# Memory tiles 4 to 15 in strips, statistics summed from strips, natural x loaded in layer 0, and a ring of six raw weight buffers

## The chip, the cores and the metric

The kernel runs on one core of one Trainium2 chip. A time is device microseconds of one execution; for the kernel before, the median of three runs is given. Shares and starts inside an execution come from one profiled execution of the same kernel, whose times are counted from the start of its span.

## The reference

Two layers of a bidirectional encoder trunk, on x of 256 tokens by 2048 and a memory of 256 tokens by 2048, all in float32:

```
for l in 0, 1:
    h    = rmsnorm(x, norm_g[l])
    proj = h @ w_in[l]                        # 2048 x 7168, split into three groups of heads
    y_a  = short gated convolution of proj's first 3072 columns
    y_d  = differential attention, 6 heads, of the next 3072 columns
    mn   = rmsnorm(mem, mem_norm_g[l])
    mkv  = mn @ w_mem_kv[l]                   # 2048 x 1024: memory keys and values
    y_m  = attention of the last 1024 columns' queries over the 256 memory tokens, gated
    x    = x + concat(y_a, y_d, y_m) @ w_out[l]
```

Two things matter for the change. The products with w_mem_kv of both layers need the memory once, transposed (contraction index on the partitions), and they don't depend on x; the kernel makes them first. And each rmsnorm needs a sum of squares per token, of mem once and of x once per layer. The kernel folds the norm's gain into the operand and applies the token's scale to the product, so these sums are needed only after the products.

## The kernel before

Every float32 product is made of three products of split operands: a number is taken apart into a high part (`hi`, in TensorE's float32r format) and the rest (`lo`), and hi*hi, hi*lo and lo*hi are accumulated in PSUM. ScalarE makes `hi` (a copy with a scale), VectorE makes `lo` (a subtraction).

**The memory stage** is the first part of the program. It has 32 steps `g`, 16 contraction tiles `k` of 128 rows for each of the two layers. A step needs 512 KB of raw weights (`weights(g)`), split by `w_parts(g)`, and for the first 16 steps the memory's tile k transposed and split into `memT` by `token_parts(g)`; `memT` is kept for layer 1's steps. `products(g, half, which)` issues twelve matmuls of 128x128x512 per step (L827): two halves (keys, values), two token blocks, three part pairs. `FIRST` is hi*hi, `REST` the other two. At step g the operands of step g + 2 are made (L942), and `beside(g)` (L856) issues loads and side work.

- Tiles 0 to 7 (`DEALT = 8`) are loaded in natural layout into `xs` (`tokens`, L774) and transposed on TensorE against an identity (`turned`, L795), two 128x128 transposes a tile.
- Tiles 8 to 15 are loaded as strips, in pieces of 512 bytes (`strips_of`, L676), four at a time, and transposed by VectorE in 32x32 blocks, one instruction of 128x1024 for four tiles (`strips_turned`, L686). The same half of mem is also loaded in natural layout, for the squares alone.
- Raw weights go through a ring of four buffers (L780): the load of step g + 4 waits until VectorE has made `lo` of step g.
- x is loaded twice in this stage: as strips for the transposed `xT` of layer 0 (`x_turned`, L692), and in natural layout (`x_natural`, L847), which gives the squares (`x_square`, L722) and is the residual to which layer 0 adds its output.
- Squares are ScalarE activations of 128x512 with an accumulated sum (`mem_squares`, L731).

**The order.** Instructions wrapped in `pin` keep the program's order on their engine; the others are placed by a planner from its own estimates. Loads go through the sync queue (SP) in order: one that waits for its buffer holds those behind it. Side work is a list of generators, `tasks`; `run_side` is called once per step or per chunk of two contraction tiles, and resumes each generator when its due chunk has come (`yield 2` means two chunks later). At the end of the stage `empty_keys` (L833) copies the keys' accumulators away on ScalarE (L836), which frees PSUM for layer 0.

**The layers.** `block` (L293) makes 16 contraction tiles of 512 columns of w_in or w_out; `load_w` (L280) has its own loads and splits (L285, L289, L290), its matmuls are L310 to L312. Blocks 0 to 5 of a layer give queries, keys, values and gate of the differential attention. From the end of block 4 on, attention runs in pairs of heads beside the blocks (`pair`, L539): scores (L593, L594), softmax, a transpose that ends with a trip through DRAM (`carry`, L424), and the product with the values (L480).

Of the kernel before, what the change touches and what calls it, by code (L numbers as in the profile page):

```python
# [19 lines left out]
P = 128  # L20
# [19 lines left out]
QT = NB // P  # L40
DEALT = 8

# [7 lines left out]
def encoder(ctx: ExitStack, tc: tile.TileContext, x, mem, norm_g, w_in, conv_w, conv_b,  # L50
# [54 lines left out]
    def small_loads():  # L105

        for m in range(DEPTH):
            yield gm_dealt[:, m], mem_norm_g[m, DEALT * P:].rearrange("(q p j) -> p q j", p=P, j=QT)
# [22 lines left out]

    gm_dealt = const.tile([P, DEPTH, (KT - DEALT) // QT, QT], F32, name="gm_dealt")

    def g_mnorm(l, k):
        if k < DEALT:
            return cva[:, l * KT + k:l * KT + k + 1]
        q, j = divmod(k - DEALT, QT)
        return gm_dealt[:, l, q, j:j + 1]

# [535 lines left out]

    def strips_of(src, at_once=1):  # L676

        st = tmp.tile([P, SEQ // B, B * QT], F32, tag="e", name=nm("xt"))
        for b in range(NA):
            pin(nc.sync.dma_start(  # L680
                st[b * B:(b + 1) * B], src[:, b * B * QT:(b + 1) * B * QT].rearrange("(n p) r -> p n r", p=B)))
            if (b + 1) % at_once == 0 and b + 1 < NA:
                yield
        return st

    def strips_turned(st):  # L686
        whole = tmp.tile([P, QT, SEQ], F32, tag="sh", name=nm("xf"))
        pin(nc.vector.transpose(whole.rearrange("p j (n i) -> p j n i", i=B),  # L688
                                st.rearrange("p n (c j) -> p j n c", j=QT)))
        return whole  # L690

    def x_turned(dst, l, q, src, at_once):  # L692


        st = yield from strips_of(src, at_once)
        yield 2
        whole = strips_turned(st)
        yield
        for j in range(QT):
            split_T(dst, q * QT + j, whole[:, j], g_norm(l, q * QT + j), pin=True)  # L700
            if j % 2:
                yield

    def x_next(dst, l, q):

        d = dram.tile([NT, P, NB], F32, name=nm("xd"))
        tc.keep_in_program_order(nc.sync.dma_start(d.rearrange("t p c -> p t c"), xs[:, :, q * NB:(q + 1) * NB]))
        yield 2
        yield from x_turned(dst, l, q, d.rearrange("t p c -> (t p) c"), NA)

# [17 lines left out]
    memT = T_tile("memT")  # L728
    ssm = const.tile([P, NT, 4], F32, name="ssm")

    def mem_squares(c):  # L731

        for t in range(NT):
            sq = tmp.tile([P, NB], F32, tag="nat", name=nm("msq"), bufs=3)
            pin(nc.scalar.activation(sq, xs[:, t, c * NB:(c + 1) * NB], AF.Square, accum_out=ssm[:, t, c:c + 1]))

    def keys(l, nat):
# [21 lines left out]
    def mem_stats():  # L759

        vec = Steps()
        t = small.tile([P, NT], F32, tag="ssum", name=nm("ssum"))
        vec.tensor_reduce(t, ssm, AX.X, ALU.add)
# [13 lines left out]
    def weights(g, at=0, n=2 * NB, eng=nc.sync):  # L777
        l, k = divmod(g, KT)
        if g not in raws:
            raws[g] = wp.tile([P, CK, NB], F32, tag="raw", name=nm("raw"), bufs=4)  # L780
        if k < DEALT:
            rows = w_mem_kv[l][k * P:(k + 1) * P]
        else:
            rows = x_row_tiles(w_mem_kv[l], k - k % CK)[:, k % CK]
        pin(eng.dma_start(raws[g].rearrange("p h c -> p (h c)")[:, at:at + n], rows[:, at:at + n]))

    def w_parts(g, at=0, n=2 * NB):
# [4 lines left out]
        pin(nc.scalar.activation(hi, raw, AF.Copy, scale=gain))  # L792
        pin(nc.vector.scalar_tensor_tensor(lo, raw, gain, hi.bitcast(F32), ALU.mult, ALU.subtract))  # L793

# [7 lines left out]

    def mem_turned(q, at_once):
        st = yield from strips_of(mem[:, q * NB:(q + 1) * NB], at_once)
        yield 2
        dealt[q] = strips_turned(st)

# [4 lines left out]
    def operands(g):  # L812
        token_parts(g)
        w_parts(g)

# [30 lines left out]

    def x_natural(c, t):  # L847
        pin(nc.sync.dma_start(xs[:, t, c * NB:(c + 1) * NB], x[t * P:(t + 1) * P, c * NB:(c + 1) * NB]))

    TOKENS = {0: 4, 1: 6, 8: 8, 9: 10, 10: 12, 11: 14}  # L850
    MEM_STRIPS = {2: 2, 4: 3}
    X_STRIPS = {12: 0, 16: 1, 20: 2, 24: 3}
    X_NATURAL = {14: (0, 0), 17: (0, 1), 20: (1, 0), 22: (1, 1), 24: (2, 0), 26: (2, 1), 28: (3, 0), 29: (3, 1)}
    X_SQUARES = {19: 0, 25: 1, 29: 2}

    def beside(g):  # L856


        if g + 4 < NG:
            if g in TOKENS:  # L860
                tokens(TOKENS[g], 2)
            weights(g + 4)
        if g in MEM_STRIPS:
            tasks.append(later(mem_turned(MEM_STRIPS[g], 2 if g == 2 else 1), 1))
        if g >= 2:
            for dst, src in islice(constants, 1):
                pin(nc.sync.dma_start(dst, src))
        if g in X_STRIPS:
            q = X_STRIPS[g]
            tasks.append(later(x_turned(xT, 0, q, x[:, q * NB:(q + 1) * NB], 1), 1))  # L870
# [8 lines left out]
        if g in X_NATURAL:  # L879
            x_natural(*X_NATURAL[g])  # L880
        if g in X_SQUARES:
            for t in range(NT):
                x_square(X_SQUARES[g], t)

    row_sums = []

    def last_square():
        for t in range(NT):
            x_square(3, t)
        yield 2  # L890
        row_sums.append(stats_of(ssx, "st"))

# [10 lines left out]
    weights(1, NB, NB)  # L903
    tokens(2, 1)
    weights(2, 0, NB)
    weights(2, NB, NB)
    tokens(3, 1)
    weights(3)
    warm(6)
    distance(0)  # L910
# [44 lines left out]
    empty_values(1)  # L955
    tasks.append(later(last_square(), 2))
    for l in range(DEPTH):
# [18 lines left out]
        for b in order:  # L976
# [185 lines left out]
```

## Time and profile before

| | |
|---|---|
| median of three runs | 918.13 us (918.06 to 918.37) |
| profiled execution, its own time | 918.26 us |
| its span | 916.5 us |
| TensorE matmul busy | 912.1 us, 4167 instructions |
| TensorE weight load busy | 758.0 us |
| VectorE busy | 682.3 us |
| ScalarE busy | 512.4 us |
| read from HBM | 194.32 MB, 235 GB/s over the span |

The busy time of TensorE counts overlapping matmuls once each as a stretch from start to modelled end, so 100% doesn't say that no time was lost between their starts; for that one looks at when successive matmuls begin. In rows of the profile, `L827 PE MATMUL acc<-hi,memT 128*128 128x512` is a matmul of the program's line 827 that writes tile `acc` from `hi` and `memT`; `x12` counts instructions; a bracket at the end gives the engine's idle time before it and what ended it. PE is TensorE, PEld its weight loads, DVE VectorE, ACT ScalarE, SP the sync engine with the loads' queue; a q behind a name means its instruction queue.

### The profile page before, as it was taken

To read this page: it belongs to the slowest core of one execution; us is meant where nothing else is said; L and a number is where in the kernel's file an instruction comes from. 1 tells how busy PE (TensorE), PEld (TensorE's weight loads), DVE (VectorE), ACT (ScalarE), POOL (GpSimd) and SP (SyncE) were. 2 spreads that over 40 slices of the span, in tenths; PEclk is the share of its full clock that TensorE was granted. 3 is DMA by queue.
4 is the path that set the end of the run, shared out by engine and by line. 5 is a ranking of instruction groups with operands and counts; after the bars stand their busy time and mean duration, and the time that the engine had idled before them with its cause. 6 is when DMAs were issued, how large, how long until landed. Compare 5 with 4: busy or idle time off the path is not lost.

```text
span 916.5 us, 12329 instructions
## 1 busy us (share of the span) xinstructions
PE 912.1 (100%) x4167; PEld 758.0 (83%) x4167; DVE 682.3 (74%) x1216; ACT 512.4 (56%) x802; POOL 7.0 (1%) x18
## 2 busy tenths in 40 slices
PE   9999999999999999999999999999999999999998
PEld 7888888888888888888888888888888888888887
DVE  5888978857897787658677757878899786658553
ACT  6766745675554765545455544568555664446431
POOL 0001000000000000000000000000000000000000
PEclk9999999999999999999999999999999999999999
DMA  9999888876769989978687867886888979978662
GB/s 286 291 270 310 273 253 235 254 211 185 187 212 239 247 249 266 264 255 249 214 257 249 237 195 221 235 237 176 242 231 222 254 206 260 288 228 241 210 216 80
DMA packets 252964, 216.11 MB, mean 236 GB/s; under 512 B 131727, under 2 KB 180197, under 8 KB 252901
## 3 DMA queue, kind: packets, MB, share of 16 engines
q1 hardware_dynamic: 250740, 211.78, 80.5%
q0 software_dynamic: 672, 2.10, 0.6%
q10 hardware_dynamic: 1488, 1.46, 0.5%
q8 instruction: 32, 0.52, 0.2%
q14 instruction: 32, 0.25, 0.1%
HBM read 194.32 MB, written 20.97 MB: 235 GB/s over the span
## 4 chain that ended last, share of the span: by engine, by line
PE 91%; DMA 4%; DVE 2%; ACT 1%; issue 1%; SPq 0%; ACTq 0%; DVEq 0%
PE acc L311 29%; PE acc L310 29%; PE acc L312 29%; DMA raw<-in_w_mem_kv_dram 3%; PE po L480 1%; PE acc L827 1%; DMA raw<-in_w_in_dram 1%; DVE xf L688 1%; DVE lo L793 1%; ACT hi L792 1%; PE poT L469 1%; PE s L594 1%; PE s L593 1%; PE s L646 1%; DMA xt<-in_mem_dram 0%
## 5 line engine op out<-in xcount | busy, mean ns | idle before, releaser
L290 DVE TENSOR_TENSOR lo<-raw,hi 128x1024 fp32r<-128x1024 f32 x288 | 351.4, 1222 | 171.0 <-ACT hi L289 167.5
L289 ACT CAST hi<-raw 128x1024 fp32r<-128x1024 f32 x288 | 302.2, 1052 | 305.5 <-PE acc L312 235.9
L311 PE MATMUL acc<-lo,xT 128*128 128x512 f32 x896 | 349.2, 390 | 0.0
L312 PE MATMUL acc<-hi,xT 128*128 128x512 f32 x896 | 348.7, 389 | 0.0
L310 PE MATMUL acc<-hi,xT 128*128 128x512 f32 x896 | 347.7, 390 | 0.2 <-ACT kraw L836 0.2
L312 PEld LDWEIGHTS acc<-hi,xT 128*128 128x128 f32 x896 | 168.2, 188 | 34.7
L310 PEld LDWEIGHTS acc<-hi,xT 128*128 128x128 f32 x896 | 168.2, 188 | 34.7 <-ACT kraw L836 0.6
L311 PEld LDWEIGHTS acc<-lo,xT 128*128 128x128 f32 x896 | 168.3, 188 | 33.7
L312 PE MATMUL acc<-hi,yT 128*128 128x512 f32 (+1 forms) x258 | 100.0, 387 | 0.0
L310 PE MATMUL acc<-hi,yT 128*128 128x512 f32 (+1 forms) x258 | 100.0, 387 | 0.0
L311 PE MATMUL acc<-lo,yT 128*128 128x512 f32 (+1 forms) x258 | 99.9, 387 | 0.0
L827 PE MATMUL acc<-hi,memT 128*128 128x512 f32 (+1 forms) x260 | 70.5, 389 | 0.0
L310 PEld LDWEIGHTS acc<-hi,yT 128*128 128x128 f32 x258 | 48.4, 188 | 10.0
L311 PEld LDWEIGHTS acc<-lo,yT 128*128 128x128 f32 x258 | 48.4, 188 | 9.9
L312 PEld LDWEIGHTS acc<-hi,yT 128*128 128x128 f32 x258 | 48.4, 188 | 9.8
L827 PEld LDWEIGHTS acc<-hi,memT 128*128 128x128 f32 x260 | 47.9, 188 | 9.8 <-ACT hi L792 0.3
L827 PE MATMUL acc<-lo,memT 128*128 128x512 f32 (+1 forms) x130 | 39.7, 387 | 0.0
L827 PEld LDWEIGHTS acc<-lo,memT 128*128 128x128 f32 x130 | 24.3, 188 | 5.0
L793 DVE SCALAR_TENSOR_TENSOR lo<-raw,cva,hi 128x1024 fp32r<-128x1024 f32 (+2 forms) x21 | 21.4, 1026 | 6.5 <-ACT hi L792 5.4
L604 ACT ACTIVATE e<-e,mx 128x256 f32<-128x256 f32 x48 | 23.8, 498 | 1.4 <-DVE mx L600 1.3
L793 DVE SCALAR_TENSOR_TENSOR lo<-raw,gm_dealt,hi 128x1024 fp32r<-128x1024 f32 x16 | 20.5, 1279 | 4.6 <-ACT hi L792 4.5
L792 ACT ACTIVATE hi<-raw,cva 128x1024 fp32r<-128x1024 f32 (+2 forms) x21 | 19.7, 947 | 6.4 <-DMA raw<-in_w_mem_kv_dram 6.4
(162 smaller groups left out, 654.6 us busy)
## 6 DMA issues: line engine op xcount, KB each, us to landing
raw<-in_w_in_dram SPq DMA_DIRECT2D x192, 512.0 KB, 4.4
raw<-in_w_out_dram SPq DMA_DIRECT2D x64, 512.0 KB, 4.7
raw<-in_w_in_dram SPq DMA_DIRECT2D x64, 256.0 KB, 4.8
raw<-in_w_mem_kv_dram SPq DMA_DIRECT2D x29, 512.0 KB, 7.1
d<-sh SPq DMA_DIRECT2D x88, 128.0 KB, 3.9
sh<-d SPq DMA_DIRECT2D x72, 128.0 KB, 3.9
xt<-in_x_dram SPq DMA_DIRECT2D x16, 128.0 KB, 6.7
xs<-in_x_dram SPq DMA_DIRECT2D x8, 256.0 KB, 6.8
```

What stands on the lines that cost most here:

```text
L289: nc.scalar.copy(hi, raw)
L290: nc.vector.tensor_tensor(lo_, raw, hi.bitcast(F32), ALU.subtract)
L310: nc.tensor.matmul(acc[t], sh, hi, start=first, stop=False)
L311: nc.tensor.matmul(acc[t], sh, lo, start=False, stop=False)
L312: nc.tensor.matmul(acc[t], sl, hi, start=False, stop=last)
L469: nc.tensor.matmul(po, vp[:, v_part, k], e[:, e_part, k], start=k + v_part + e_part == 0, stop=k == NT - 1 and v_part == 1)
L480: nc.tensor.matmul(po[:, t, :], eT[:, i, t, k, :], v[:, k, h * P:(h + 1) * P], start=k == 0, stop=k == NT - 1)
L593: nc.tensor.matmul(s[c][:, i, :], qi, k_first(yT, c, h), start=True, stop=False)
L604: nc.scalar.activation(e[:, c, i], e[:, c, i], AF.Exp, bias=mx[:, c, i:i + 1], accum_out=sm[:, c, i:i + 1])
L792: pin(nc.scalar.activation(hi, raw, AF.Copy, scale=gain))
L793: pin(nc.vector.scalar_tensor_tensor(lo, raw, gain, hi.bitcast(F32), ALU.mult, ALU.subtract))
L827: pin(nc.tensor.matmul(accs[l, half][t][:, at:at + n], memT[:, token_part, k, t * P:(t + 1) * P], p, start=k == 0 and at == 0 and token_pa ...
```

## The change

- Only tiles 0 to 3 are transposed on TensorE (`DEALT = 4`). Tiles 4 to 7 come as two pairs of strips, in pieces of 256 bytes (`mem_pair`), tiles 8 to 15 as strips of 512-byte pieces as before. VectorE turns the strips tile by tile (`mem_turn`), called from `w_parts` between its `hi` and its `lo`; `token_parts` of a tile now follows its `w_parts`. Strips are loaded into parts of `xs`.
- Natural rows of mem are loaded for tiles 0 to 3 alone; the other squares are taken from the strips, in activations of 128x128 (`strip_squares`), whose sums are spread over partitions and brought together by 16 small copies on VectorE (`folded`). x's squares for layer 0 are made in the same way.
- The raw weights of the memory stage go through six buffers: two are the homes of tiles that layer 0 uses later (`mqT`, `mga`). The load of step g + 6 waits for `lo` of step g.
- x's strips start at steps 9, 13, 17 and 21 instead of 12, 16, 20 and 24, are turned in two halves, and x's natural rows are loaded from the end of block 4 of layer 0, eight loads of 256 KB, one every second chunk.
- The gains of tiles 4 to 15 come as rows dealt to partitions; the first of these small loads is issued before the stage's loop.

```diff
-DEALT = 8
+DEALT = 4
+PAIRED = 8
+RING = 6
...
-    def strips_turned(st):
-        whole = tmp.tile([P, QT, SEQ], F32, tag="sh", name=nm("xf"))
+    def turn_strips(whole, st, at, n, of=QT):
         pin(nc.vector.transpose(whole.rearrange("p j (n i) -> p j n i", i=B),
-                                st.rearrange("p n (c j) -> p j n c", j=QT)))
-        return whole
+                                st.rearrange("p n (c j) -> p j n c", j=of)[:, at:at + n]))
...
+    def strip_squares(which, q, st, ns):
+        for n in ns:
+            v = st(n)
+            sq = tmp.tile([P, NB], F32, tag="nat", name=nm("ssq"), bufs=3)
+            o = sq[:, 0:P]
...
+            pin(nc.scalar.activation(o, v, AF.Square, accum_out=strip_sums[which][:, q, n:n + 1]))
+
+    def folded(vec, which, dst, at):
+        sums = strip_sums[which]
+        nq = sums.shape[1]
+        for a in range(NA):
+            for c in range(NA):
+                vec.tensor_copy(dst[c * B:(c + 1) * B, :, at + a * nq:at + (a + 1) * nq],
+                                sums[a * B:(a + 1) * B].rearrange("p q (t c) -> p c t q", c=NA)[:, c])
...
-            raws[g] = wp.tile([P, CK, NB], F32, tag="raw", name=nm("raw"), bufs=4)
+            if g % RING < 4:
+                raws[g] = wp.tile([P, CK, NB], F32, tag="raw", name=nm("raw"), bufs=4)
+            else:
+                raws[g] = keep.tile([P, CK, NB], F32, tag=("mqT", "mga")[g % RING - 4], name=nm("raw"))
...
         pin(nc.scalar.activation(hi, raw, AF.Copy, scale=gain))
+        if turn is not None:
+            mem_turn(turn)
         pin(nc.vector.scalar_tensor_tensor(lo, raw, gain, hi.bitcast(F32), ALU.mult, ALU.subtract))
...
+    def mem_pair(j):
+        k = DEALT + 2 * j
+        for _ in strips_in(pairs[j], mem[:, k * P:(k + 2) * P], NA):
+            pass
...
+    def mem_turn(k):
+        q, j = divmod(k, QT)
+        if j == 0:
+            dealt[q] = whole_tile()
+        if k < PAIRED:
+            turn_strips(dealt[q][:, j:j + 1], pairs[j // 2], j % 2, 1, 2)
+        else:
+            turn_strips(dealt[q][:, j:j + 1], mem_in[q], j, 1)
...
+    def x_first(q):
+        st = x_in[q]
+        yield from strips_in(st, x[:, q * NB:(q + 1) * NB])
         yield 2
-        dealt[q] = strips_turned(st)
+        whole = whole_tile()
+        for j in range(0, QT, 2):
+            turn_strips(whole[:, j:j + 2], st, j, 2)
+            strip_squares("x", q, lambda i: st[:, i], range(j * 2, j * 2 + 4))
+            yield
+            for i in (j, j + 1):
+                split_T(xT, q * QT + i, whole[:, i], g_norm(0, q * QT + i), pin=True)
+            if j == 0:
+                yield
...
     def operands(g):
-        token_parts(g)
-        w_parts(g)
+        if g == DEALT:
+            w_parts(g, 0, NB, turn=g)
+            token_parts(g)
+            w_parts(g, NB, NB)
+        else:
+            w_parts(g, turn=g if DEALT <= g < KT else None)
+            token_parts(g)
...
-    TOKENS = {0: 4, 1: 6, 8: 8, 9: 10, 10: 12, 11: 14}
-    MEM_STRIPS = {2: 2, 4: 3}
-    X_STRIPS = {12: 0, 16: 1, 20: 2, 24: 3}
-    X_NATURAL = {14: (0, 0), 17: (0, 1), 20: (1, 0), 22: (1, 1), 24: (2, 0), 26: (2, 1), 28: (3, 0), 29: (3, 1)}
-    X_SQUARES = {19: 0, 25: 1, 29: 2}
+    MEM_STRIPS = {2: 2, 5: 3}
+    X_STRIPS = {9: 0, 13: 1, 17: 2, 21: 3}
+    MEM_SQUARES = {4: 2, 5: 2, 6: 2, 7: 2, 8: 3, 9: 3, 10: 3, 11: 3, 12: 4}
...
-        if g + 4 < NG:
-            if g in TOKENS:
-                tokens(TOKENS[g], 2)
-            weights(g + 4)
+        if g == 0:
+            mem_pair(1)
+            weights(5)
+        if g + RING < NG:
+            weights(g + RING)
...
-        if g in (4, 8, 11, 13):
-            mem_squares((4, 8, 11, 13).index(g))
+        if g == 3:
+            mem_squares(0)
+        mem_strip_squares(MEM_SQUARES.get(g, 0))
...
+    def x_natural():
+        for c in range(KT // QT):
             for t in range(NT):
-                x_square(X_SQUARES[g], t)
...
+                pin(nc.sync.dma_start(xs[:, t, c * NB:(c + 1) * NB], x[t * P:(t + 1) * P, c * NB:(c + 1) * NB]))
+                yield 2
...
-    tokens(2, 1)
+    tokens(2, 2)
     weights(2, 0, NB)
     weights(2, NB, NB)
-    tokens(3, 1)
     weights(3)
+    mem_pair(0)
+    constant()
+    weights(4)
...
-    tasks.append(later(last_square(), 2))
+    tasks.append(later(x_sums(), 1))
...
             if b == 4:
                 start = chunk[0]
+                if l == 0:
+                    tasks.append(later(x_natural(), 1))
```

More of the change, by code (lines that the diff above doesn't have):

```diff
@@ L674, in encoder, with strips_in, whole_tile, x_turned @@
     mem_done = set()
-    def strips_of(src, at_once=1):
-        st = tmp.tile([P, SEQ // B, B * QT], F32, tag="e", name=nm("xt"))
+    def strips_in(st, src, at_once=1, apart=1):
+        n = st.shape[-1]
         for b in range(NA):
             pin(nc.sync.dma_start(
-                st[b * B:(b + 1) * B], src[:, b * B * QT:(b + 1) * B * QT].rearrange("(n p) r -> p n r", p=B)))
+                st[b * B:(b + 1) * B], src[:, b * n:(b + 1) * n].rearrange("(n p) r -> p n r", p=B)))
             if (b + 1) % at_once == 0 and b + 1 < NA:
-                yield
-        return st
-    def strips_turned(st):
-        whole = tmp.tile([P, QT, SEQ], F32, tag="sh", name=nm("xf"))
+                yield apart
+    def whole_tile():
+        return tmp.tile([P, QT, SEQ], F32, tag="sh", name=nm("xf"))
+    def turn_strips(whole, st, at, n, of=QT):
         pin(nc.vector.transpose(whole.rearrange("p j (n i) -> p j n i", i=B),
-                                st.rearrange("p n (c j) -> p j n c", j=QT)))
-        return whole
-    def x_turned(dst, l, q, src, at_once):
-        st = yield from strips_of(src, at_once)
+                                st.rearrange("p n (c j) -> p j n c", j=of)[:, at:at + n]))
+    def x_turned(dst, l, q, src):
+        st = tmp.tile([P, SEQ // B, B * QT], F32, tag="e", name=nm("xt"))
+        yield from strips_in(st, src, NA)
         yield 2
-        whole = strips_turned(st)
+        whole = whole_tile()
+        turn_strips(whole, st, 0, QT)
         yield
@@ L708, in x_next @@
         yield 2
-        yield from x_turned(dst, l, q, d.rearrange("t p c -> (t p) c"), NA)
+        yield from x_turned(dst, l, q, d.rearrange("t p c -> (t p) c"))
     def stats_of(parts, tag):
@@ L728, in encoder @@
     memT = T_tile("memT")
-    ssm = const.tile([P, NT, 4], F32, name="ssm")
+    ssm = const.tile([P, NT, 4 * NA], F32, name="ssm")
     def mem_squares(c):
@@ L801, in encoder, with area, mem_strips, mem_strip_squares @@
     dealt = {}
-    def mem_turned(q, at_once):
-        st = yield from strips_of(mem[:, q * NB:(q + 1) * NB], at_once)
-        yield 2
-        dealt[q] = strips_turned(st)
+    def area(t, at, n, r):
+        return xs[:, t, at:at + n].rearrange("p (n r) -> p n r", r=r)
+    pairs = [area(0, D_MODEL // 2 + j * NB, NB, 2 * B) for j in range(2)]
+    mem_in = {2: area(1, D_MODEL // 2, D_MODEL // 2, P), 3: area(0, 0, D_MODEL // 2, P)}
+    x_in = [area(t, at, D_MODEL // 2, P) for t, at in ((0, D_MODEL // 2), (1, D_MODEL // 2), (0, 0), (1, 0))]
+    def mem_pair(j):
+        k = DEALT + 2 * j
+        for _ in strips_in(pairs[j], mem[:, k * P:(k + 2) * P], NA):
+            pass
+    def mem_strips(q):
+        yield from strips_in(mem_in[q], mem[:, q * NB:(q + 1) * NB], 2)
+    def mem_turn(k):
[6 more added lines that the diff above has]
+            turn_strips(dealt[q][:, j:j + 1], mem_in[q], j, 1)
+    both_pairs = xs[:, 0, D_MODEL // 2:].rearrange("p (s n r) -> p n s r", s=2, r=2 * B)
+    mem_sums = [(q, n) for q in range(3) for n in range(NW)]
+    def mem_strip_squares(n):
+        for _ in range(n):
+            q, at = mem_sums.pop(0)
+            strip_squares("m", q, lambda i: both_pairs[:, i] if q == 0 else mem_in[q + 1][:, i], [at])
+    def x_first(q):
+        st = x_in[q]
+        yield from strips_in(st, x[:, q * NB:(q + 1) * NB])
+        yield 2
+        whole = whole_tile()
+        for j in range(0, QT, 2):
[6 more added lines that the diff above has]
+                yield
     def token_parts(g):
@@ L878, in beside, with x_sums @@
             tasks.append(later(rest_of_constants(), 1))
-        if g in X_NATURAL:
-            x_natural(*X_NATURAL[g])
-        if g in X_SQUARES:
-            for t in range(NT):
-                x_square(X_SQUARES[g], t)
[L885 to L891, printed above, removed]
+    row_sums = []
+    def x_sums():
+        vec = Steps()
+        folded(vec, "x", ssm, 0)
+        yield from vec.run(8)
+        row_sums.append(stats_of(ssm, "st"))
+    def x_natural():
+        for c in range(KT // QT):
+            for t in range(NT):
+                pin(nc.sync.dma_start(xs[:, t, c * NB:(c + 1) * NB], x[t * P:(t + 1) * P, c * NB:(c + 1) * NB]))
+                yield 2
     for _ in range(DEPTH):
```

34 lines of the change are left out of this document (21 added, 13 removed).

## The prediction, made before the changed kernel had run

> **What bounds the kernel now.** I read the page's engine shares first, then the clock row, then who waited for whom on TensorE.
>
> ```profile
> span 916.5 us, 12329 instructions
> ...
> PE 912.1 (100%) x4167; PEld 758.0 (83%) x4167; DVE 682.3 (74%) x1216; ACT 512.4 (56%) x802; POOL 7.0 (1%) x18
> ...
> PEclk9999999999999999999999999999999999999999
> ...
> PE warm L125 <- PEq L1148: 0.8, 1, 0.8
> PE acc L310 <- ACT kraw L836: 0.2, 1, 0.2
> ```
>
> The clock is full throughout, and in the whole span TensorE is seen waiting twice, 1.0 us together. Busy time alone would not prove saturation, because matmuls overlap. So I looked at starts: in TensorE's timeline of the memory stage I marked where each token tile begins (its first pair of products, or the group that opens with it).
>
> ```profile
> 14.28 0.62 PE L827 MATMUL acc<-hi,memT 128*128 128x512 f32 x2
> 14.74 0.60 PE L798 MATMUL pt<-ident,xs 128*128 128x128 f32 x4
> ...
> 17.50 0.62 PE L827 MATMUL acc<-hi,memT 128*128 128x512 f32 x2
> 17.95 0.38 PE L798 MATMUL pt<-ident,xs 128*128 128x128 f32 x2
> ...
> 20.49 0.62 PE L827 MATMUL acc<-hi,memT 128*128 128x512 f32 x2
> 20.95 0.38 PE L798 MATMUL pt<-ident,xs 128*128 128x128 f32 x2
> ...
> 23.48 1.07 PE L827 MATMUL acc<-hi,memT 128*128 128x512 f32 x4
> ...
> 26.20 1.07 PE L827 MATMUL acc<-hi,memT 128*128 128x512 f32 x4
> ```
>
> These are the starts of tiles 3 to 7. A tile is 12 products and takes 2.72 us where nothing stands between them (23.48 to 26.20), 0.227 us a product. TensorE is therefore fed without a gap, and the program's time is its count of matmuls plus its few gaps. Whatever the change does to DMA, ScalarE or VectorE counts only if it removes a matmul, removes a gap, or makes one.
>
> **The change part by part: what leaves TensorE.** Tiles 4 to 7 lose their eight identity transposes (L798). Their price is the excess over 2.72: tile 3, which carries the four of tiles 4 and 5, takes 17.50 - 14.28 = 3.22 (0.50 more); tile 4, with tile 6's two, takes 2.99 (0.27 more); tile 5, with tile 7's two, takes 2.99 (0.27 more). Sum 1.04 us. Nothing is added to TensorE.
>
> The Trainium skill, "TensorE: Matmul & The Clock Gate", Part 4: PE-mode transpose, gives about 275 ns for one 128x128 transpose in a kernel; by it eight would be worth 2.2 us. The durations above agree (0.38 us covers two overlapping ones), the spacing of the tiles does not, and the sum goes by the spacing.
>
> **The gap that may leave.** The second wait stands at the border to layer 0, here in the timelines of TensorE, ScalarE and the sync queue:
>
> ```profile
> 94.17 0.61 PE L827 MATMUL acc<-lo,memT 128*128 128x512 f32 x2
> 94.96 0.50 PE L310 MATMUL acc<-hi,xT 128*128 128x512 f32 x1 [0.17 <-ACT kraw L836]
> 95.30 0.39 PE L311 MATMUL acc<-lo,xT 128*128 128x512 f32 x1
> ...
> 91.39 1.05 ACT L289 CAST hi<-raw 128x1024 fp32r<-128x1024 f32 x1 [2.42 <-DMA raw<-in_w_in_dram]
> ...
> 94.33 1.07 ACT L836 COPY kraw<-acc 128x512 f32<-128x512 f32 x2
> ...
> 82.85 13.23 SPq L285 DMA_DIRECT2D raw<-in_w_in_dram  x6
> ```
>
> The last memory product starts at 94.17 + 0.23 = 94.40, the next at 94.96: 0.56 instead of 0.227, 0.33 lost; the one after comes 0.34 later, 0.11 lost. Together 0.44 us. The accumulators are emptied late (kraw, L836) because the copy stands on ScalarE behind a cast that waited 2.42 us for layer 0's weights. Those were late because the DMA engines were full:
>
> ```profile
> 65.00:80.00 15.00, 15.00 (x67) 12.14 (x66) 14.03 (x32) 8.74 (x16) 1.18 (x2) 1.00 1.06 271
> 80.00:95.00 15.00, 14.83 (x67) 11.95 (x65) 12.72 (x14) 10.31 (x18) 1.72 (x4) 1.00 1.03 349
> ...
> 225.00:240.00 15.00, 15.00 (x74) 12.64 (x73) 9.82 (x10) 8.48 (x16) 0.00 (x0) 1.00 0.67 199
> ```
>
> (The last two columns are DMA share and GB/s; before them come PE, PEld, DVE, ACT, POOL and the clock.) The change takes natural mem of tiles 8 to 15 (1 MB) and natural x (2 MB) out of this stage: 3 MB at 271 GB/s is some 12 us of full engines out of 95. The ring of six also lets layer 0's first load into its buffer two tiles (5.4 us) sooner. I take the gap as gone, 0.44, and keep 0 as the other end. I can't see what could be late next: xT's last tile is split three tiles earlier than before.
>
> **What must stay hidden: VectorE at tiles 4 to 6.** Its work there has a new start. Durations and spacing come from its timeline and ScalarE's, and from the lines' groups:
>
> ```profile
> 14.57 0.75 DVE L793 SCALAR_TENSOR_TENSOR lo<-raw,cva,hi 128x512 fp32r<-128x512 f32 x1 [0.20 <-ACT hi L792]
> ...
> 18.15 1.28 DVE L793 SCALAR_TENSOR_TENSOR lo<-raw,cva,hi 128x1024 fp32r<-128x1024 f32 x1
> 19.34 0.42 DVE L262 TENSOR_TENSOR memT<-pt,memT 128x256 fp32r<-128x256 f32 x1
> ...
> 24.02 2.00 DVE L688 STREAM_TRANSPOSE xf<-xt 128x1024 f32<-128x1024 f32 x1
> ...
> 241.31 0.70 DVE L554 STREAM_TRANSPOSE sh<-e 128x512 f32<-128x512 f32 x1
> ...
> 16.73 1.17 ACT L792 ACTIVATE hi<-raw,cva 128x1024 fp32r<-128x1024 f32 x1
> ...
> 19.69 0.62 ACT L735 ACTIVATE msq<-xs 128x512 f32<-128x512 f32 x1
> L619 ACT ACTIVATE hsq<-po x24: 255/268/278, 255.5 to 732.5; 128x128 f32<-128x128 f32 x24
> L619 ACT ACTIVATION_READ_ACCUMULATOR hsq<-po x24: 190/196/204, 255.7 to 732.6; 128x1 f32 x24
> L189 DVE TENSOR_SCALAR ss<-ss,stm x4: 224/226/230, 59.2 to 101.7; 128x4 f32<-128x4 f32 x4
> ```
>
> One turned tile is 128x256, a shape the trace lacks. Half of the contiguous 128x512 gives 0.35 us, a quarter of the strided 2.00 gives 0.50; a fixed part of 0.15 on top would make 0.65. The new read is strided, so 0.50. VectorE's queue after lo of tile 3 (ends 15.3): turn 4 to 15.8, first half of lo to 16.6, memT's low part to 17.0, second half to 17.7, turn 5 to 18.2, lo to 19.5, memT low to 19.9. With the transposes gone tile 5 starts at 14.28 + 2 x 2.72 = 19.72, and its first product with memT's low part two products later, 20.17. That is 0.3 us of cover, the thinnest place (0.65 for each turn leaves none). From there VectorE needs 0.50 + 1.19 + 0.42 = 2.1 a tile against 2.72 and draws ahead, unless ScalarE holds it: natural squares stay at tile 3 (2 x 0.62), which puts hi of tile 6 near 19.7 to 20.8, lo to 22.1, memT low to 22.5, needed at 22.44 + 0.45 = 22.9. Both hold; uncovered, each tenth late is a tenth lost.
>
> ScalarE: 56 small squares come (0.27 to 0.46 each, the read beside the next or not: 15 to 26 us), 14 large ones go (0.62: 8.7 us). Net 6 to 17 us over a stage where it is busy seven tenths; cost zero beside lookahead. VectorE: four turns (2 us), ten more cuts of turns it did whole (1.5 at 0.15), 32 fold copies at up to 0.23 (7 us). Half of the folds fall near tile 13, half (3.7 us) at layer 0's start, ahead of lo splits there; but x's last turn of 2.0 us and its splits leave that place for three tiles earlier. From 80 to 95 us VectorE had 2.3 us of 15 idle. I take 0, with up to 1.7 (3.7 less 2.0) as the other end.
>
> **Loads.** The pair strips are pieces of 256 bytes, the mem and x strips of 512, and memT 4's come behind weights 3 instead of whole rows of 1 KB. The issue rows bound them:
>
> ```profile
> L785 SPq DMA_DIRECT2D raw<-in_w_mem_kv_dram x2: 328/328/328, 5.7 to 7.1; - x2
> ...
> DMA to landing us min/median/max: 5.4/5.7/6.1
> ...
> 18.79 0.58 SPq L680 DMA_DIRECT2D xt<-in_mem_dram  x1
> ...
> sh<-d SPq DMA_DIRECT2D x72, 128.0 KB, 3.9
> xt<-in_x_dram SPq DMA_DIRECT2D x16, 128.0 KB, 6.7
> ```
>
> Weights 3 and 4 landed at 11.1 and 13.2 (issued 5.7, 7.1). Four pair issues of some 0.45 us and a gain vector put weights 4 at about 8.6, a landing near 14; ScalarE is busy with tile 3 until about 14.5 either way (it released the lo of 14.57). 128 KB in pieces of 128 bytes lands in 3.9 us, no later than pieces of 512 in a busier stage. So the pair is there by 13, needed at 15.3. The last of tile 8's strips was issued at 18.8; it now stands behind weights 9, which wait for lo of tile 3 (15.3), so near 17. Tile 8 starts at 14.28 + 5 x 2.72 = 27.9, so its turn may begin as late as 26.
>
> The Trainium skill, "DMA: Bandwidth & Descriptors", Specifications, says that moves under 512 bytes miss line rate, being read, modified and written. It speaks against the pairs; the row of 128-byte pieces disagrees, and even doubled the pair would land inside the 2 us of margin.
>
> **The sum.** The profiled execution took 918.26 us (span 916.5, 1.76 around it), 0.13 over the median 918.13. 918.26 - 1.04 - 0.44 = 916.78; as a median 916.65.
>
> **Rivals.**
> 1. *The border gap stays*: its DMA share was still 1.03, and 349 GB/s flowed. Then 918.13 - 1.04 = 917.1.
> 2. *New waits at tiles 4 to 8*: turns of 0.65, each strip a microsecond late, or the folds uncovered. Against it, the margins above; for it, that they were made of estimates. 0.5 to 1.9 us lost: 917.2 to 918.6.
> 3. *Slower: x's natural rows jam layer 0's first attention pair.* They are eight 256 KB loads on the sync queue, one in two chunks (5.4 us) from the end of block 4, near 195 to 240 us on that queue; right behind comes the pair's carry through DRAM (242.05), whose result feeds the po matmuls:
>
> ```profile
> 242.05 1.78 SPq L429 DMA_DIRECT2D d<-sh  x4
> L480 PEldq EVENT_SEMAPHORE  x2: 51/51/51, 251.2 to 251.8; - x2
> 254.31 1.06 PE L480 MATMUL po<-v,sh 128*128 128x128 f32 x8
> ```
>
> TensorE's weight queue passed its wait at 251.8 and the product ran at 254.31: 2.5 us of cover, and from there each microsecond counts. Four loads still ahead are 1.05 MB at 199 GB/s, 5.3 us, 2.8 lost: 919.5. All eight are 10.5 us, 8 lost: 924.7. Against it: DMA share was 0.67 there, so each load should be gone before the next.
> 4. *A transpose is worth its duration*: 8 x 0.27 = 2.2 us in place of 1.04, and the gap: 915.5. The tile starts speak against it.
> 5. *Not what it says*: there is no wait on weights on TensorE for a ring of six to take away; that is in the sum already.
>
> **How the numbers follow.** Forecast 0.59; rival 1 0.14; rival 2 0.10; rival 3 0.12, most of it with more than four loads; rival 4 0.05. Its own range is 916.65 less twice the runs' spread of 0.31, 916.0. The upper end takes rivals 1 and 2 and the half case of 3, 919.5; outside lie the full case and rival 4. About 0.2% (1.84 us) is what a measurement of this kernel can tell from no change: below 916.3 counts as faster, above 920.0 as slower. Faster: rival 4 and the lowest part of the forecast, 0.11. Slower: the heavier part of rival 3, 0.10. The rest, 0.79.
>
> **What would show it.** Right: no L798 after tile 3, tile starts 2.72 apart from tile 3 on, layer 0's first product 0.23 after the last memory product with casts no longer waiting for its weights, DMA share well under 1 after 50 us, and layer 0 as long as before. Wrong: TensorE waiting for turn or memT at 17 to 29 us (rival 2), for po at 250 to 330 (rival 3), or a stage that shrinks by 2 us.

## The result: 1.2% slower

| | before | after |
|---|---|---|
| median of four runs | 918.1 us (917.98 to 918.37) | 928.58 us (927.55 to 929.92) |
| profiled execution, its own time | 918.26 us | 929.29 us |
| its span | 916.5 us | 927.5 us |

The ratio is 1.0115, 95% interval 1.0097 to 1.0132. The forecast was 916.7, with a range of 916.0 to 919.5: not even the sign was right. (Below, "before" and "after" also name the profiled executions of the two kernels.) The page of the changed kernel and who waited for whom on TensorE:

```profile
span 927.5 us, 12460 instructions
...
PE 916.5 (99%) x4159; PEld 758.9 (82%) x4159; DVE 688.7 (74%) x1263; ACT 520.9 (56%) x887; POOL 7.0 (1%) x18
...
PE acc L911 <- ACT mv L926: 4.0, 1, 4.0
PE acc L911 <- ACT memT L264: 2.5, 2, 2.1
PE warm L129 <- PEq L1236: 0.8, 1, 0.8
PE acc L911 <- DVE memT L265: 0.3, 1, 0.3
```

Eight matmuls are gone (4167 to 4159), and four new waits have come, 6.8 us together. All stand in the memory stage: layer 0's first product starts at 106.33 us instead of 94.96, 11.37 later, and from there to the end of the span after is the shorter by 0.3 us. Read as tile starts in TensorE's timeline:

```profile
18.25 1.55 PE L911 MATMUL acc<-hi,memT 128*128 128x512 f32 x4 [0.40 <-ACT memT L264]
...
24.59 1.07 PE L911 MATMUL acc<-hi,memT 128*128 128x512 f32 x4
...
27.31 1.07 PE L911 MATMUL acc<-hi,memT 128*128 128x512 f32 x4
...
29.58 0.61 PE L911 MATMUL acc<-lo,memT 128*128 128x512 f32 x2
32.25 0.81 PE L911 MATMUL acc<-hi,memT 128*128 128x512 f32 x2 [2.06 <-ACT memT L264]
...
58.52 0.63 PE L911 MATMUL acc<-lo,memT 128*128 128x512 f32 x2
63.17 2.22 PE L911 MATMUL acc<-hi,memT 128*128 128x512 f32 x4 [4.02 <-ACT mv L926]
...
105.88 0.62 PE L911 MATMUL acc<-lo,memT 128*128 128x512 f32 x2
106.33 0.39 PE L313 MATMUL acc<-hi,xT 128*128 128x512 f32 x1
```

These are the starts of tiles 4, 6, 7, 8 (32.25), 17 (63.17) and of layer 0 (106.33), with what stands right ahead of the long waits. A tile is here twelve products in the order of their issue; where layer 1 begins, the keys' products of steps 16 and 17 come first, so that "tile 17" is the values' products of both steps. Tiles 8 and 17 of before:

```profile
28.92 1.07 PE L827 MATMUL acc<-hi,memT 128*128 128x512 f32 x4
...
53.40 1.07 PE L827 MATMUL acc<-hi,memT 128*128 128x512 f32 x4
```

Against the starts of before: tile 7 is 1.11 us late although 1.04 us of transposes are gone, so tiles 0 to 6 lost 2.15. Tiles 8 and 9 lose 4.27 more, tiles 17 and 18 another 6.33. The border gives 0.34 back. 1.11 + 4.27 + 6.33 - 0.34 = 11.37.

Both large losses are longer than their waits. The windows of the trace show why (columns: stretch, its length, busy time and count of PE, PEld, DVE, ACT and POOL, granted TensorE clock, DMA share, GB/s):

```profile
29.00:32.50 3.50, 1.44 (x7) 0.90 (x6) 1.37 (x2) 0.71 (x4) 0.00 (x0) 1.00 1.10 278
32.75:36.15 3.40, 3.15 (x8) 2.28 (x8) 3.04 (x6) 3.32 (x9) 0.00 (x0) 0.50 1.06 203
36.20:58.00 21.80, 21.80 (x97) 17.83 (x96) 19.88 (x42) 18.13 (x58) 0.00 (x0) 1.00 1.04 272
58.80:63.40 4.60, 0.58 (x3) 0.19 (x1) 3.39 (x11) 2.50 (x8) 0.00 (x0) 1.00 1.10 270
63.50:66.85 3.35, 3.33 (x8) 2.48 (x8) 2.09 (x4) 3.08 (x5) 0.00 (x0) 0.50 0.69 192
67.00:90.00 23.00, 23.00 (x102) 18.74 (x101) 21.64 (x48) 16.46 (x49) 0.37 (x1) 1.00 0.71 208
```

After each of the two waits the granted clock is 0.50 for some 3.4 us, in which 8 products start instead of 15. The first wait made tile 8 late by 2.22 us, the half clock added 2.05 by tile 9; the second 4.39 and 1.94. It isn't one execution's accident: the mean granted clock is 0.996 in all four executions of after and 1.0 in the profiled one of before. The page's clock row, in slices of 23 us, shows nothing but nines.

**Why tile 17 waits for mv.** ScalarE's `mv` (L926) scales the values by the memory's statistics and so empties accumulators that TensorE wants next. VectorE's and ScalarE's timelines of after:

```profile
49.77 1.37 DVE L192 COPY ssm<-sums 32x6 f32<-32x6 f32 x8
...
54.05 1.41 DVE L192 COPY ssm<-sums 32x6 f32<-32x6 f32 x8
...
57.51 0.17 DVE L192 TENSOR_REDUCE ssum<-ssm 128x2 f32<-128x26 f32 x1
...
62.16 0.17 DVE L192 COPY stm<-rsy 128x2 f32<-128x2 f32 x1
```

```profile
48.40 1.15 ACT L827 ACTIVATE hi<-raw,cva 128x1024 fp32r<-128x1024 f32 x1
52.99 0.31 ACT L754 ACTIVATE ssq<-xs 128x128 f32<-128x128 f32 x1 [3.44 <-issue]
...
62.43 1.26 ACT L926 ACTIVATE mv<-acc,stm 128x512 f32<-128x512 f32 x2 [2.10 <-DVE stm L192]
```

And the same of before:

```profile
44.49 0.15 DVE L189 TENSOR_REDUCE ssum<-ssm 128x2 f32<-128x8 f32 x1
...
48.17 0.17 DVE L189 COPY stm<-rsy 128x2 f32<-128x2 f32 x1
...
50.99 1.27 ACT L842 ACTIVATE mv<-acc,stm 128x512 f32<-128x512 f32 x2
```

`mem_stats` is a list of small VectorE operations that is resumed once a step and issues eight each time. Before, it had 15, two resumptions, 3.9 us from end to end. The 16 folds make it 31, four resumptions, with an `lo` or a turn between them: 12.6 us. The folds themselves are short (0.17 us each, 2.8 us in all); what is late is the fourth resumption. Besides, ScalarE stood 3.44 us at the squares of x's first strips, with the next `hi` behind them.

**Why tiles 3 to 8 are late.** The sync queue's issues in after, and who made it wait up to 40 us:

```profile
5.99 2.44 SPq L683 DMA_DIRECT2D xs<-in_mem_dram  x4
9.75 0.39 SPq L937 DMA_DIRECT2D gm_dealt<-in_mem_norm_g_dram  x1
10.43 0.35 SPq L820 DMA_DIRECT2D raw<-in_w_mem_kv_dram  x1
11.35 3.35 SPq L683 DMA_DIRECT2D xs<-in_mem_dram  x4
14.74 2.72 SPq L820 DMA_DIRECT2D raw<-in_w_mem_kv_dram  x4
...
21.76 1.57 SPq L683 DMA_DIRECT2D xs<-in_mem_dram  x2
...
SPq L683 <- DMA raw<-in_w_mem_kv_dram: 6.2, 5, 2.2
SPq L820 <- DMA raw<-in_w_mem_kv_dram: 5.4, 5, 1.5
```

Weights 4 were issued at 10.43 instead of the 8.6 forecast, weights 5 at 14.74 (9.37 before), the last of tile 8's strips at 21.76 and after instead of near 17. The queue waits for landings of loads that have nothing to do with the buffer it is about to fill. Where landings can be matched to issues, each held issue begins as the eighth load before it lands (11.35 behind a landing at 11.33, 14.25 behind one at 14.22), so I read it as eight loads under way at most; that is worked out from the trace, and no run tests it. In the trace these loads tell of their landing by eight semaphores, used almost strictly in turn, so the limit may be the program's own and not the queue's. The same windows of before and after:

```profile
10.00:15.00 5.00, 5.00 (x27) 4.03 (x26) 3.00 (x6) 2.60 (x5) 0.00 (x0) 1.00 1.05 401
```

```profile
10.00:15.00 5.00, 4.89 (x24) 3.61 (x23) 2.59 (x5) 3.11 (x6) 0.00 (x0) 1.00 1.02 218
```

The DMA engines are as full as before and move 218 GB/s in place of 401. ScalarE and VectorE then wait for what comes late:

```profile
17.18 0.72 ACT L827 ACTIVATE hi<-raw,gm_dealt 128x512 fp32r<-128x512 f32 x1 [1.94 <-DMA raw<-in_w_mem_kv_dram]
...
31.13 0.63 DVE L692 STREAM_TRANSPOSE xf<-xs 128x256 f32<-128x256 f32 x1 [4.52 <-DMA xs<-in_mem_dram]
```

### The profile page after: what moved, and what is told of

It reads as the page before. It is cut to its first block, busy times and chain, and to the rows that moved or that the text cites. A ratio compares the mean times of both kernels' runs of the same rounds, so it can differ in the third digit from the quotient of the medians.

```text
span 927.5 us, 12460 instructions
## 1 busy us (share of the span) xinstructions
PE 916.5 (99%) x4159; PEld 758.9 (82%) x4159; DVE 688.7 (74%) x1263; ACT 520.9 (56%) x887; POOL 7.0 (1%) x18
## 4 chain that ended last, share of the span: by engine, by line
PE 94%; DMA 4%; ACT 1%; DVE 1%; SPq 0%; issue 0%
PE acc L314 28%; PE acc L315 28%; PE acc L313 28%; PE acc L911 6%; DMA raw<-in_w_mem_kv_dram 2%; PE po L483 1%; DMA xs<-in_mem_dram 1%; PE poT L472 1%; PE s L597 1%; PE s L596 1%; PE s L649 1%; DMA xs<-in_x_dram 0%; ACT hi L827 0%; ACT ssq L754 0%; DVE lo L830 0%; DVE xf L692 0%
## 5 line engine op out<-in xcount | busy, mean ns | idle before, releaser
L911 PE MATMUL acc<-hi,memT 128*128 128x512 f32 (+1 forms) x260 | 74.1, 403 | 7.0 <-ACT mv L926 4.0
L830 DVE SCALAR_TENSOR_TENSOR lo<-raw,gm_dealt,hi 128x1024 fp32r<-128x1024 f32 (+1 forms) x25 | 30.8, 1234 | 5.0 <-ACT hi L827 4.8
L827 ACT ACTIVATE hi<-raw,gm_dealt 128x1024 fp32r<-128x1024 f32 (+1 forms) x25 | 27.6, 1105 | 2.4 <-DMA raw<-in_w_mem_kv_dram 2.4
L754 ACT ACTIVATE ssq<-xs 128x128 f32<-128x128 f32 x56 | 16.6, 298 | 6.5 <-issue 3.4
```

What stands on the lines that cost most here:

```text
L754: pin(nc.scalar.activation(o, v, AF.Square, accum_out=strip_sums[which][:, q, n:n + 1]))
L911: pin(nc.tensor.matmul(accs[l, half][t][:, at:at + n], memT[:, token_part, k, t * P:(t + 1) * P], p, start=k == 0 and at == 0 and token_pa ...
```

## The experiments

The expectations use these theories. *S*: the statistics are late because their list grew. *X*: ScalarE's stand at x's first squares makes them late. *O*: tile 8's strips are late because of their place in the sync queue. *B*: the added loads in small pieces slow the DMA engines, wherever they stand. *Q*: the added loads take places in the queue, whatever their pieces. Unless a number of executions is given, a kernel ran once, beside the kernel before at 918.5 to 918.9 on the same chip. "Late" means against the same start in before.

**The statistics in two resumptions.**

```
-        yield from vec.run(8)
+        yield from vec.run(16)
```

> The changed kernel with one number changed: the memory statistics' 31 VectorE operations are issued in two steps of 16 instead of four of 8. In the changed kernel TensorE waits 4.0 us at tile 17 for mv (L926), and tile 17 and 18 together start 6.3 us later against the kernel before than tile 16 did. Theory S (the steps make the statistics late): two steps fewer are 5.4 us, the wait for mv falls under 1 us, no slow clock after it, the time falls by 5 to 6.3 us to about 923 to 924.5. Rival X (the queues of ScalarE and VectorE are held there by the wait for x's first strips, 3.4 us at 49.5): the wait stays over 2 us and the time falls by less than 3 us. Tile 8 stays as it is under both.

Measured: 922.09 us, 7.2 less than the profiled execution of after. TensorE's waits:

```profile
PE acc L911 <- ACT memT L264: 0.9, 1, 0.9
...
PE acc L911 <- DVE lo L830: 0.8, 1, 0.8
PE acc L911 <- DVE memT L265: 0.7, 2, 0.3
PE acc L911 <- ACT kraw L920: 0.3, 1, 0.3
```

No wait for mv, no half clock. From tile 15 to 18 the loss is 2.27 us instead of 6.32: S holds for about two thirds of it. Of the rest 0.8 is a wait for `lo`, which stands on VectorE behind the longer resumption. Tiles 8 and 9, which the edit doesn't touch, also lost less here (1.85 for 4.27): their strips came a little earlier in this run, and no half clock followed the wait of 0.9 us. So of the 7.2 us some 4.1 are the edit's own.

**x's strips three steps later.**

```
-    X_STRIPS = {9: 0, 13: 1, 17: 2, 21: 3}
+    X_STRIPS = {12: 0, 16: 1, 20: 2, 24: 3}
```

> The changed kernel with x's strips at steps 12, 16, 20 and 24, as in the kernel before, instead of 9, 13, 17 and 21. Rival X: the 3.4 us wait of ScalarE at 49.5 goes, and with it at least 3 us of TensorE's wait at tile 17; time about 923 to 925. Theory S: the statistics still come in four steps; the wait for mv falls by less than 2 us, time 927 to 929. The tile 8 wait stays under both.

Measured: 924.55 us. The wait for mv shrinks from 4.0 to 2.4 us, and tiles 17 and 18 lose 4.58 instead of 6.33. X is real, worth 1.7 us here, and second to S: the wait fell by 1.6, not by the 3 that X had asked. The time lies where X put it only because 3.0 of the 4.7 us came at tiles up to 9, which the edit doesn't touch (tile 9 is 2.36 us late for 5.39 in after).

**Tile 8's strips ahead of the second pair.**

```
-    MEM_STRIPS = {2: 2, 5: 3}
+    MEM_STRIPS = {0: 2, 5: 3}
```

> The changed kernel with the strips of tiles 8 to 11 issued from step 0 on instead of step 2, so ahead of weights 7 and 8 on the sync queue. In the changed kernel VectorE waits 4.5 us for these strips and TensorE loses 4.3 us at tiles 8 and 9 (2.2 us idle, the rest at half clock). Theory O (order: they stand behind weights 8 and 9, which six buffers let go ahead): the wait at tile 8 goes and no half clock follows; tiles 8 and 9 lose under 0.5 us, at most 1 us is lost earlier on weights 7 or 8. Rival B (the engines move too little from 10 to 30 us because of the 256-byte pieces, whatever the order): as much is lost in another place between tiles 5 and 9, over 2 us in all.

Measured: 929.79 us. VectorE no longer waits for the strips of tile 8; it waits 1.55 us for `hi` in that place, and so for weights. Tiles 5 and 6 lost 1.56 to weights, and from tile 4 to tile 9 2.2 us went in all, as B had it. Tile 9 is 2.35 us late, which is 3.0 less than in after but no less than in the two kernels above, whose strips stand where they stood (2.24 and 2.36). Tile 16, with a new wait of 2.6 us for kraw, lost 2.8 more. O falls as a cure: moved up, the strips make something else late.

**A ring of four.**

```
-RING = 6
+RING = 4
```

(with the first loads in the order that four buffers need)

> The changed kernel with a ring of four raw buffers as before: the load of step g + 4 waits for lo of step g, and weights 4 stand behind the first pair and ahead of the second. Theory O: weights 8 and 9 no longer stand ahead of the strips of tiles 8 to 11, which land 3 us sooner; the loss at tiles 8 and 9 falls from 4.3 us to under 1 us. Rival B: it stays over 3 us. Both: tile 17 as in the changed kernel, the border to layer 0 may lose up to 0.4 us again.

Measured: 929.75 us. The border's 0.33 us stays gone. Tiles 8 and 9 lose 2.68, between the under 1 of O and the over 3 of B, and tiles 17 and 18 8.5. So the ring of six makes neither the gain nor the losses.

**No pairs: tiles 4 to 7 natural and transposed on TensorE, the rest of the change kept.**

```
-DEALT = 4
+DEALT = 8
...
-            mem_pair(1)
+            tokens(6, 2)
...
-    mem_pair(0)
+    tokens(4, 2)
```

> The changed kernel with tiles 4 to 7 as in the kernel before: two loads of 256 KB in natural rows and eight transposes on TensorE instead of the two pairs of strips; their squares natural. Everything else of the change stays (six buffers, strip sums for tiles 8 to 15 and x, natural x in layer 0). In the four runs so far the changed kernel lost between 2.2 and 4.3 us from tile 4 to tile 9 wherever the strips of tile 8 stood, and with four buffers as with six. Theory B (the pairs' 256-byte pieces slow the loads of the first 30 us): tiles 4 to 9 lose under 0.7 us against the kernel before, with tile 8's strips in time; tile 17 still waits for mv. Rival R (strips one by one behind the weights, turned tile by tile, whatever tiles 4 to 7 do): tile 8 still loses over 1.5 us.

Measured: 926.83 us. From tile 2 to tile 9 nothing is lost (0.60 us late at tile 2, 0.65 at tile 9; 0.72 follows at tile 10, for strips). The statistics are as late as in after (4.6 us of wait for mv, tiles 17 and 18 lose 7.6). So the early losses, the wait at tile 8 among them, come with the pairs; the edit takes their turns and squares away with their loads, and the added loads further down tell these apart.

**Both cures, with and without the pairs.** The two edits of the first experiments together, once on the kernel without pairs, once on the changed kernel.

> The kernel without pairs, with the statistics in two steps of 16 and x's strips at steps 12, 16, 20, 24. Each of the last two alone took 4.0 and 1.7 us off the loss at tile 17 in the changed kernel. If pairs, statistics' steps and x's strips are the whole loss: no wait over 0.5 us, no half clock, the memory stage as long as in the kernel before, the border gap gone: 917.3 to 918.0, 0.1 to 0.8 us faster than the kernel before on this chip. If something else of the change costs (the small squares on ScalarE, natural x in layer 0): over 919.

> The changed kernel, pairs kept, with the statistics in two steps of 16 and x's strips at steps 12, 16, 20, 24. If tile 17's loss has just these two causes it goes: the time is the kernel before plus what is lost up to tile 9 (2.2 to 2.4 us where no half clock follows) less 0.4 at the border: 919.5 to 921. If the squares of x and the keys' squares on ScalarE still hold mv: 921 to 923.

Measured in 10 and 9 executions: without pairs 920.29 us, ratio 1.0014 (1.0003 to 1.0026); with pairs 922.08, ratio 1.0034 (1.0024 to 1.0044). The pairs, which were to gain 1.04, cost 1.8 us even with the rest mended. Without pairs 917.3 to 918.0 was expected if the named causes were all, and 920.29 says that they aren't. In its profiled execution 1.7 us go at tiles 9 and 10, where VectorE waits for the strips, and 1.1 behind tile 16; with pairs 2.06 go from tile 15 to 18, only 0.2 less than with the statistics' edit alone, so S and X don't add. There TensorE no longer waits for mv, but with pairs:

```profile
PE acc L911 <- DVE lo L830: 1.8, 1, 1.8
```

The second resumption, now 15 operations in a row and 2.8 us long, stands on VectorE ahead of the `lo` that TensorE wants. Taken together in fewer steps, the operations are done sooner and hold up what stands behind them.

**What is it in the pairs?** To the kernel without pairs come eight loads of 64 KB that nobody reads, in the pairs' places on the queue: once in the pairs' pieces of 256 bytes, once in pieces of 2 KB to 32 partitions. A third kernel loads tiles 4 to 7 as one set of four loads in pieces of 512 bytes.

```
+        for _ in strips_in(dummy[j], mem[:, (4 + 2 * j) * P:(6 + 2 * j) * P], NA):
+            pass
```

```
+        for b in range(NA):
+            pin(nc.sync.dma_start(dummy[j][b * B:(b + 1) * B].rearrange("p n r -> p (n r)"),
+                                  mem[b * B:(b + 1) * B, j * NB:(j + 1) * NB]))
```

```
-PAIRED = 8
+PAIRED = 4
...
+        for _ in strips_in(mem_in[1], mem[:, NB:2 * NB], NA):
```

> The kernel without pairs (e6_nopair), with eight loads of 64 KB added that nobody reads, in pieces of 256 bytes to 32 partitions each, four ahead of weights 4 and four ahead of weights 5: the pairs' loads beside the natural ones. Theory B (the 256-byte pieces cost the engines time): the first 30 us get dear again; tiles 4 to 9 lose over 2 us where they lost none without pairs, and at least 1.5 us more than with the same bytes in pieces of 2 KB (e13_dummy2k). Rival Q (eight more loads, at most some eight of which can be under way, keep the queue from running ahead, whatever their pieces): both kernels lose the same within 0.7 us.

> The same kernel with the eight added loads of 64 KB in pieces of 2 KB to 32 partitions each: as many loads, as many bytes, an eighth of the pieces. Theory B: tiles 4 to 9 lose under 1 us against the kernel without pairs. Rival Q: as much as with pieces of 256 bytes, over 2 us.

> The changed kernel with tiles 4 to 7 loaded as one set of strips of 512-byte pieces, four loads of 128 KB ahead of weights 4, instead of two pairs of 256-byte pieces in eight loads of 64 KB; everything else as changed, the statistics in four steps too. Theory B and rival Q both expect the loads to run faster; B by half the pieces, Q by half the loads. Tile 4's weights come some 1 us later since all four tiles' strips stand ahead. From tile 4 to tile 9 1 to 2 us are lost (2.2 to 4.3 with pairs). Tile 17 loses its 4 to 6 us again.

Measured: 933.03, 932.82 and 928.34 us. The total isn't the measure here, since later waits and half clocks follow from the early delay. Nor is the stretch up to tile 9 that the expectations name: tile 9 is 6.97 us late with the 256-byte pieces and 6.03 with the 2 KB pieces, less apart than B asked, but only the latter has a half clock of 3.4 us in it. Tile 7's start, chosen after the result, has none in either. It is 0.65 us late without added loads, 2.32 with the 2 KB pieces, 4.97 with the 256-byte pieces. The window that was 401 and 218 above, in this order:

```profile
10.00:15.00 5.00, 5.00 (x25) 3.86 (x25) 2.84 (x5) 3.18 (x6) 0.00 (x0) 1.00 1.06 390
```

```profile
10.00:15.00 5.00, 5.00 (x26) 4.06 (x25) 3.11 (x6) 2.82 (x6) 0.00 (x0) 1.00 1.08 260
```

```profile
10.00:15.00 5.00, 4.90 (x24) 3.62 (x23) 2.71 (x5) 2.99 (x6) 0.00 (x0) 1.00 1.16 234
```

Eight more loads of 0.5 MB together cost 1.7 us in pieces of 2 KB, so B alone doesn't hold; the small pieces cost 2.65 more, so Q alone doesn't either. Both work, by one run each. By the traces' packets of these windows a piece of 256 bytes kept its DMA engine 31 ns and one of 2 KB 140 ns, 8 and 15 bytes per ns. One rival is left untested: every added load writes 32 partitions, a load of natural rows 128, and no run varies that. Tiles 4 to 7 as one set, half as many loads in pieces twice as long, lose 1.77 us from tile 4 to tile 9, as expected, but that is no clear gain: the six kernels with pairs lose 1.48 to 4.63 there, and the window moved 219 GB/s, against 218 to 264 with them.

**A version that keeps what works.** No pairs; statistics in two resumptions, one step earlier; the memory's squares four a step; x's strips late; strips of tiles 8 to 15 a step earlier.

```
-    MEM_STRIPS = {2: 2, 5: 3}
+    MEM_STRIPS = {1: 2, 4: 3}
-    MEM_SQUARES = {8: 3, 9: 3, 10: 3, 11: 3, 12: 4}
+    MEM_SQUARES = {8: 4, 9: 4, 10: 4, 11: 4}
-        if g == 13:
+        if g == 12:
```

> The kernel without pairs, with the statistics in two steps one step earlier (from step 12, the small squares done by step 11), x's strips at steps 12, 16, 20, 24 and the strips of tiles 8 to 15 one step earlier. The kernel e8_nopair_stats_xlate still lost 1.7 us at tiles 9 and 10 to late strips and 1.1 us at tile 17 to the statistics. If these two have been named rightly, both fall under 0.5 us and the time is 917.4 to 918.6 beside a kernel before of 918.1 to 918.6: the same within 0.1%, at best 0.4 us faster (the border gap). If strips cost whatever their place: 919.5 or more.

Measured in 10 executions: 920.2 us, ratio 1.0018 (1.0009 to 1.0028). Both losses that it was to mend are gone, and 917.4 to 918.6 was still missed. TensorE waits for nothing in the stage, which still ends 0.77 us late: 0.83 are lost before tile 1, and tiles 15 and 16 start 0.28 later. Two more went after the start and after the 0.7 us that `po` waited here: the first restores the order in which before loads tiles 2 and 3, the second also loads x's natural rows from the end of block 1 on.

```
-    tokens(2, 2)
+    tokens(2, 1)
...
+    tokens(3, 1)
```

```
+            if l == 0 and b == 1:
+                tasks.append(later(x_natural(), 1))
```

> The kernel of e10_best, in which TensorE no longer waits in the memory stage, with the first natural tiles loaded as in the kernel before: tile 2 ahead of weights 2, tile 3 behind them, instead of both ahead. In every changed kernel so far tile 1 started 0.1 to 1.4 us later than in the kernel before, because the second half of weights 0 landed at 6.1 to 6.6 us instead of 5.5. If the doubled load at 3.2 us does that, tile 1 starts within 0.2 us of the kernel before and the time falls by some 0.5 us to 919.5 or less; if it is the chip or chance, tile 1 stays 0.4 to 0.8 late and the time at 920.

> The same, with x's natural rows loaded from the end of block 1 of layer 0 instead of block 4. The kernel of e10_best lost 0.7 us at 315 us, where the product of the third attention pair waited for its trip through DRAM. If natural x (rival 3 of the prediction, in a small form) or the order that the planner made with it is the cause, this wait goes: 0.5 to 0.8 us less than e14_tokens. If not, the same as e14_tokens within 0.3 us. Either would be the first version not slower than the kernel before: 918.0 to 919.0.

Measured in 11 executions each: 919.7 us, ratio 1.0014 (1.0004 to 1.0023), and 919.58, ratio 1.0012 (1.0003 to 1.0021), above the 918.0 to 919.0 that was expected. The profiled execution of the second, its fastest, took 918.63, with a single wait of TensorE in the whole trace:

```profile
span 916.9 us, 12451 instructions
...
PE warm L129 <- PEq L1235: 0.8, 1, 0.8
```

There every tile from 1 to 31 stands 0.6 us behind before and the border gap is gone, so the stage ends 0.25 late; in the first of the two, tile 1 was 2.6 us late and no tile behind it lost more. The order of tiles 2 and 3 is thus not what delays the start. Neither of the two waits for `po`, so moving x's natural rows isn't shown to do anything. Their executions spread from 918.5 to 922.6, and those of before on the same chip from 917.95 to 919.7. None of the versions beats the kernel before.

## Why the prediction was wrong

*What leaves TensorE* was right as far as the runs show it. In after, tiles 3 to 5 held waits; in the changed kernel with both cures tile 3 takes 2.73 and tile 4 2.72, 0.49 and 0.27 less than before, and the kernels without pairs keep their spacing of before. Tile 5, which waits in every kernel with pairs, takes 0.26 less in the one with a single set of strips. Rival 4 falls: its price for tile 3 would be 1.1.

*The gap that may leave* was right too: 0.34 us at layer 0's first product and 0.45 by its second, for 0.44. It goes in every variant, the ring of four among them, so the larger ring isn't what closes it; the DMA share is 0.71 from 67 to 90 us, as that step reasoned, but no run tries this by itself.

*What must stay hidden: VectorE at tiles 4 to 6*: the turn took 0.44 us for the 0.50 taken. Products of tiles 4 and 5 did wait some tenths for memT's low part (0.5 us each at their weight loads), but VectorE had itself stood idle for `hi` just before, 1.56 and 0.43 us. The cover that I counted in tenths was never tested, because the weights came microseconds late.

*VectorE's folds* are the step that failed most. "I take 0, with up to 1.7" counted their durations against VectorE's idle time. 32 at up to 0.23 was even too much (0.17). What I never asked is who waits for the statistics and how their list is paced: what was late next was the fourth resumption, then mv, then TensorE's accumulators, at tile 17, 6.33 us. Every row for it stood in the trace of before: the 15 operations, the two resumptions, mv 2.7 us behind the last of them.

*ScalarE's squares* ("cost zero beside lookahead") failed in the same way: their duration was hidden, their wait for x's strips was not, and the next `hi` stood behind it (1.7 us alone, 0.2 once the list is in two resumptions).

*Loads* failed second. The sum of issue times put weights 4 at 8.6 and tile 8's strips near 17, on a queue that issues every 0.45 us. That the queue also holds issues for landings of other loads was to be seen in before, in its waits up to 40 us, and I didn't ask why:

```profile
SPq L785 <- DVE lo L793: 5.5, 5, 2.6
SPq L680 <- DMA raw<-in_w_mem_kv_dram: 3.1, 2, 1.9
```

The first row is the ring of four, which the change relieves; the second has nothing to do with it.

And "128 KB in pieces of 128 bytes lands in 3.9 us" compared a quiet stage with one in which the DMA engines are full: there the pairs' loads took the place of weights. I had cited the Trainium skill, "DMA: Bandwidth & Descriptors", Specifications, on moves under 512 bytes, and let the 3.9 us row overrule it. The 256-byte and the 2 KB runs side by side (2.65 us at tile 7) say that its rule bears here; that 512 bytes are enough in this stage they don't say, and the set in pieces of 512 moved 219 GB/s.

*Rival 2* had the place (tiles 4 to 8) and half the mechanism, strips late; at 0.5 to 1.9 us it was mis-sized, against 2.15 up to tile 7 and 4.27 behind it. *Rival 3*, the one that was to be slower, did not happen: TensorE has no wait for `po` in after. Two of the kernels without pairs waited 0.6 and 0.7 us for it; why, stays open. *Rival 5* was right as far as the ring goes.

One term is missing altogether, a stall's price beyond itself. Some 4 of the 11 us are half clock, and no part of the sum had a place for it. That the wait of 2.06 us met the clock as it did was partly chance, as the last section shows.

## What to carry to other kernels

For each value that a change computes in another way, find its last consumer in the trace and count when it is ready: operations, resumptions, what stands between them. A duration that fits into an engine's idle time says nothing of that. On a stage where the DMA engines are full and one queue issues everything, another load is paid for by the loads behind it, in number as well as in the size of its pieces. Fewer, longer steps on VectorE finish a side task sooner but hold up the splits behind them. And a stall of 2 us on a saturated TensorE may cost 4.

## What the runs showed of the hardware

- A wait of 2.06 us ahead of tile 8 was followed by 3.4 us at half clock, as was one of 4.02 us; one of 2.63 us ahead of tile 16 (the kernel with tile 8's strips first) was not. So the length alone doesn't decide. In the traces' clock marks the slow stretches last 3.41 or 6.83 us and begin on a grid of 3.413 us: in after the full clock begins at 5.45 us, the slow stretches at 32.75 and 63.47, 8 and 17 such steps later. With TensorE's waits laid on that grid, all ten steps at full clock with 1.76 us or more of waiting are followed by half clock, and none with 1.58 or less. The place decides with the length: 1.76 us inside one step halved the clock (the 2 KB pieces, ahead of tile 8); 1.76 cut by a step into 1.14 and 0.62 did not (the pairs with both cures, at tile 17), nor did the 2.63, cut into 1.05 and 1.58. These are waits up to the profile's modelled ends of products. The Trainium skill, "TensorE: Matmul & The Clock Gate", Part 1: The HAM clock gate, has a free-running window of 3413 ns. The grid agrees with it; that the clock falls only after an idle window of about 3.4 us does not agree with the 2.06, nor with the 1.76.
- A turn of 128x256 took VectorE 0.44 us from a strip of two tiles and 0.63 from a strip of four: the same elements, read at twice the stride.
- The start of the stage moves by chance: tile 1 began 0.1 to 2.6 us later than in the profiled execution of before, over kernels whose first loads are nearly alike. What decides it stays open, and it is as large as the gains that were sought.
